# Filling a constant in 55 steps and bringing gamma over GpSimd's queue, in an RMSNorm and SiLU kernel

## The chip, the cores and the metric

The kernel runs on one core of a Trainium2 chip. The metric is the device time of one execution in microseconds. Three runs of the kernel before gave 316.87 to 317.08 us, with a median of 317.0 us.

## The reference

```
x: (8, 1024, 2048) f32, gamma: (2048,) f32, eps = 1e-5
rms = sqrt(mean(x ** 2, axis=-1) + eps)
out = gamma * x / rms
return out * (1 / (1 + exp(-out)))
```

Each of the 8192 rows of 2048 elements is normalised by its root mean square, multiplied by gamma and put through SiLU. The input and the output are 67.1 MB each.

## The kernel before

The 8192 rows are cut into 16 blocks of 512 rows. A block is one tile `xt` of 128 partitions, with four rows of x (J = 4), or 32 KB, in each partition. Six such tiles rotate (BUFS = 6), so that a block's tile can be loaded again only when the store of the block six before is done. The results are written over the block's own tile.

For each block, the squares of each row are summed by ScalarE for one or two of the four rows (L77) and by VectorE for the others (L83). ScalarE takes the square root (L89), VectorE the reciprocal (L94), VectorE multiplies the block by gamma (L99), and ScalarE applies SiLU with the reciprocal as its scale (L104). After the first block, the square root and the reciprocal are made for two blocks at a time.

Loads are issued from ScalarE's queue (L56), stores from SP's (L106). The order of all instructions is written out by hand under `manual_schedule`, so each engine and each queue takes its work in the order of the source. From block 6 on, a load stands behind the first row of squares of the block two before it.

The start is what the change touches. Gamma must stand in all 128 partitions of the tile `g`, because VectorE multiplies by it. Its 8 KB are loaded to partition 0 of `g` over SP's queue (L113). VectorE fills the 128 x 128 tile `ones` (L110) and the tile `eps_t` (L111). TensorE multiplies a row of ones by gamma, in four matmuls of 512 columns, into the PSUM tile `junk_v` (L116); each is two passes in the profile. VectorE copies `junk_v` to `g` (L118). ScalarE has a small activation that reads one column of `ones` (L112) and a small copy of one column of `junk_v` (L119). The loads of blocks 0 and 1 are issued ahead of that last copy, and those of blocks 2 to 5 behind it:

```
load(1)
nc.vector.tensor_copy(out=g, in_=junk_v)
nc.scalar.copy(out=junk_a[:, 0:1], in_=junk_v[:, d - 1:d])
for b in range(2, BUFS):
    load(b)
```

`junk_v` is also where VectorE's sums of squares put their unused products, so these stand behind the copy as well.

Of the kernel before, what the change touches and what calls it, by code (L numbers as in the profile page):

```python
# [1 line left out]

# [4 lines left out]

ACT = mybir.ActivationFunctionType
ALU = mybir.AluOpType


@with_exitstack
def kernel(
    ctx: ExitStack,
    tc: tile.TileContext,
    x: bass.AP,
    gamma: bass.AP,
    eps: bass.AP,
    out: bass.AP,
):  # L20

    nc = tc.nc
    P = nc.NUM_PARTITIONS
    f32 = mybir.dt.float32
    x2 = x.flatten_outer_dims()
    o2 = out.flatten_outer_dims()
    n, d = x2.shape
    J = 4
    BUFS = 6
    nblk = n // (P * J)  # L30
    last = nblk - 1
    xb = x2.rearrange("(b p j) d -> b p (j d)", p=P, j=J)
    ob = o2.rearrange("(b p j) d -> b p (j d)", p=P, j=J)

    GROUPS = [(0,)] + [(b, b + 1) for b in range(1, last, 2)] + [(last,)]

    singles = ctx.enter_context(tc.tile_pool(name="singles", bufs=1))
    pool = ctx.enter_context(tc.tile_pool(name="pool", bufs=BUFS))
    small = ctx.enter_context(tc.tile_pool(name="small", bufs=3))
    psum = ctx.enter_context(tc.tile_pool(name="psum", bufs=1, space=bass.MemoryType.PSUM))  # L40

    Q = 4
    w = d // Q
    g = singles.tile([P, d], f32)
    eps_t = singles.tile([P, 1], f32)
    ones = singles.tile([P, P], f32)
    junk_a = psum.tile([P, d], f32, name="junk_a")
    junk_v = psum.tile([P, d], f32, name="junk_v")
    blocks, sums, scales, place = {}, {}, {}, {}
    for q in GROUPS:  # L50
        for k, b in enumerate(q):
            place[b] = (q, k * J)

    def load(b):
        xt = pool.tile([P, J * d], f32, name="xt")
        nc.scalar.dma_start(out=xt, in_=xb[b])  # L56
        blocks[b] = xt

    def row(b, j):
        return blocks[b][:, j * d:(j + 1) * d]  # L60

    def share(b):
        if b == last:
            return 1
        return 1 if b in ONE else 2

    ONE = (5, 9, 13)

    def total(b, j):
        q, at = place[b]  # L70
        if q not in sums:
            sums[q] = small.tile([P, J * len(q)], f32, name="ss")
        return sums[q][:, at + j:at + j + 1]

    def squares_scalar(b):
        for j in range(share(b)):
            nc.scalar.activation(out=junk_a, in_=row(b, j), func=ACT.Square, accum_out=total(b, j))  # L77
            if j == 0 and BUFS <= b + 2 < nblk and b >= J:
                load(b + 2)

    def squares_vector(b):
        for j in range(share(b), J):
            nc.vector.tensor_tensor_reduce(  # L83
                out=junk_v, in0=row(b, j), in1=row(b, j), scale=1.0, scalar=0.0,
                op0=ALU.mult, op1=ALU.add, accum_out=total(b, j))

    def root(q):
        rms = small.tile([P, J * len(q)], f32, name="rms")
        nc.scalar.activation(out=rms, in_=sums.pop(q), func=ACT.Sqrt, scale=1.0 / d, bias=eps_t)  # L89
        scales[q] = rms  # L90

    def invert(q):
        rstd = small.tile([P, J * len(q)], f32, name="rstd")
        nc.vector.reciprocal(out=rstd, in_=scales[q])  # L94
        scales[q] = rstd

    def by_gamma(b, lo=0, hi=J):
        part = blocks[b][:, lo * d:hi * d].rearrange("p (j d) -> p j d", d=d)
        nc.vector.tensor_mul(out=part, in0=part, in1=g.unsqueeze(1).to_broadcast([P, hi - lo, d]))  # L99

    def silu(b):
        q, at = place[b]
        for j in range(J):
            nc.scalar.activation(out=row(b, j), in_=row(b, j), func=ACT.Silu,  # L104
                                 scale=scales[q][:, at + j:at + j + 1])
        nc.sync.dma_start(out=ob[b], in_=blocks[b])  # L106

    with tc.manual_schedule():
        load(0)
        nc.vector.memset(ones, 1.0)  # L110
        nc.vector.memset(eps_t, float(eps))  # L111
        nc.scalar.activation(out=junk_a[:, 0:1], in_=ones[:, 0:1], func=ACT.Square)  # L112
        nc.sync.dma_start(out=g[0:1, :], in_=bass.AP(tensor=gamma.tensor, offset=gamma.offset, ap=[[d, 1], [1, d]]))  # L113
        for c in range(Q):
            cols = slice(c * w, (c + 1) * w)
            nc.tensor.matmul(junk_v[:, cols], ones[0:1, :], g[0:1, cols], start=True, stop=True)  # L116
        load(1)
        nc.vector.tensor_copy(out=g, in_=junk_v)  # L118
        nc.scalar.copy(out=junk_a[:, 0:1], in_=junk_v[:, d - 1:d])  # L119
        for b in range(2, BUFS):  # L120
            load(b)

        q = GROUPS[0]
        squares_scalar(0)
        squares_vector(0)
        root(q)
        by_gamma(0)
        invert(q)

        q = GROUPS[1]  # L130
        squares_scalar(1)
        squares_vector(1)
        silu(0)
        squares_scalar(2)
        squares_vector(2)
        root(q)
        by_gamma(1)
        invert(q)
        by_gamma(2)
        silu(1)  # L140

        for q in GROUPS[2:-1]:
            a, c = q
            if a == 3:
                squares_scalar(a)
                silu(a - 1)
            else:
                silu(a - 1)
                squares_scalar(a)
            squares_vector(a)  # L150
            by_gamma(a)
            squares_scalar(c)
            squares_vector(c)
            root(q)
            invert(q)
            by_gamma(c)
            silu(a)

        q = GROUPS[-1]
        silu(last - 1)  # L160
        squares_scalar(last)
        squares_vector(last)
        root(q)
        by_gamma(last, 0, J // 2)
        invert(q)
        by_gamma(last, J // 2, J)
        silu(last)


# [1 line left out]
_INS = ['x', 'gamma', 'eps']  # L171
_OUTS = [((8, 1024, 2048), 'float32')]

_NUMBERS = {'eps': 9.999999747378752e-06}


# [26 lines left out]
```

## Time and profile before

| | |
|---|---|
| median of three runs | 317.0 us (316.87 to 317.08) |
| profiled execution, its time | 317.02 us |
| profiled execution, its span | 315.2 us |
| VectorE busy | 226.5 us, 72% of the span |
| ScalarE busy | 204.8 us, 65% |
| TensorE, GpSimd busy | 7.2 us, 0.2 us |
| DMA | 134.24 MB, mean 426 GB/s |
| a load, 4096 KB, from issue to landing | 38.6 us (median) |
| a store, 4096 KB, from issue to landing | 36.9 us (median) |

The span runs from the first instruction to the last; the profiled execution's time is longer by 1.8 us, which lie around the span. All durations in the text are from this one execution. A line such as L116 is a line of the kernel's file. The engines are PE (TensorE), PEld (its weight loads), DVE (VectorE), ACT (ScalarE), POOL (GpSimd) and SP (SyncE); a q behind the name means the engine's queue of instructions or transfers.

### The profile page before, as it was taken

The numbers are of one execution on the slowest core, as the hardware profiler recorded it, in microseconds if no ns is written. First come the engines' busy times: TensorE is split into PE (matmuls) and PEld (weight loads), VectorE is DVE, ScalarE is ACT, GpSimd is POOL, SyncE is SP. The second block draws the span as 40 slices with busy tenths as digits, with TensorE's granted clock in tenths as the row PEclk, the third lists the DMA queues.
The fourth block names the chain that finished last, engine by engine and source line by source line (L and its number), as shares of the span: only waits on it lengthen the run. The fifth ranks groups of instructions, "written<-read, shape, count | busy, mean of one in ns | idle before, by whom it ended". The sixth has DMA issues, their size and how long they took to land.

```text
span 315.2 us, 407 instructions
## 1 busy us (share of the span) xinstructions
PE 7.2 (2%) x8; PEld 2.5 (1%) x8; DVE 226.5 (72%) x101; ACT 204.8 (65%) x150; POOL 0.2 (0%) x4
## 2 busy tenths in 40 slices
PE   6200000000000000000000000000000000000000
PEld 2000000000000000000000000000000000000000
DVE  0699999997798584685949669466795957859400
ACT  1169959977970699606993079950899108995800
POOL 0000000000000000000000000000000000000000
DMA  8999999999999999999999999999999999999997
GB/s 334 407 457 412 412 437 403 462 403 463 403 457 407 457 407 462 403 458 407 457 407 457 412 453 412 457 407 457 412 453 412 453 412 453 420 449 416 449 424 308
DMA packets 4612, 134.24 MB, mean 426 GB/s; under 512 B 513, under 2 KB 513, under 8 KB 513
## 3 DMA queue, kind: packets, MB, share of 16 engines
q10 hardware_dynamic: 2304, 67.11, 49.8%
q1 hardware_dynamic: 2306, 67.12, 49.3%
q14 instruction: 2, 0.02, 0.0%
HBM read 67.12 MB, written 67.11 MB: 426 GB/s over the span
## 4 chain that ended last, share of the span: by engine, by line
DMA 68%; ACT 11%; DVE 11%; PE 2%; issue 1%; ACTq 1%; another core or an unknown queue 0%; DVEq 0%
DMA xt<-in_x_dram 68%; ACT xt L104 9%; DVE xt L99 5%; DVE junk_v L83 4%; PE junk_v L116 2%; ACT junk_a L77 1%; DVE g L118 1%; DMA g<-in_gamma_dram 1%; ACTq L198 1%; ACT L104 0%; ACT L89 0%; DVE ss L83 0%; ACT rms L89 0%; DVE rstd L94 0%
## 5 line engine op out<-in xcount | busy, mean ns | idle before, releaser
L99 DVE TENSOR_TENSOR xt<-xt,g 128x8192 f32<-128x8192 f32 (+1 forms) x17 | 138.9, 8170 | 6.9 <-ACT junk_a L77 6.6
L104 ACT ACTIVATE xt<-xt,rstd 128x2048 f32<-128x2048 f32 x64 | 122.3, 1989 | 5.3 <-DVE rstd L94 4.8
L83 DVE CUSTOM_DVE_ANT_0 junk_v<-xt 128x2048 f32<-128x2048 f32 x36 | 82.7, 2299 | 41.2 <-DMA xt<-in_x_dram 40.5
L77 ACT ACTIVATE junk_a<-xt 128x2048 f32<-128x2048 f32 x28 | 52.5, 1875 | 69.4 <-DMA xt<-in_x_dram 67.2
L89 ACT ACT_TABLE_LOAD x9 | 11.5, 1283 | 7.9 <-DVE ss L83 7.9
L104 ACT ACT_TABLE_LOAD x9 | 11.5, 1283 | 0.2
L94 DVE RECIPROCAL rstd<-rms 128x8 f32<-128x8 f32 (+1 forms) x9 | 1.7, 194 | 10.2 <-ACT rms L89 10.2
L118 DVE COPY g<-junk_v 128x2048 f32<-128x2048 f32 x1 | 2.3, 2292 | 9.1 <-PE junk_v L116 9.1
L116 PE MATMUL junk_v<-g,ones 1*128 1x512 f32 x8 | 7.2, 1072 | 2.9 <-DMA g<-in_gamma_dram 2.9
L119 ACT COPY junk_a<-junk_v 128x1 f32<-128x1 f32 x1 | 0.1, 144 | 9.9 <-DVE g L118 9.9
L77 ACT ACTIVATION_READ_ACCUMULATOR junk_a<-xt 128x1 f32 x28 | 5.2, 187 | 0.0
L83 DVE DVE_READ_ACCUMULATOR2_ANT ss<- 128x1 f32 x36 | 5.1, 140 | 0.0
L89 ACT ACTIVATE rms<-ss,eps_t 128x8 f32<-128x8 f32 (+1 forms) x9 | 2.7, 300 | 0.1
L116 PEld LDWEIGHTS junk_v<-g,ones 1*128 1x128 f32 x8 | 2.5, 325 | 6.0 <-issue 6.0
L112 ACT ACT_TABLE_LOAD x1 | 1.3, 1283 | 1.1 <-PEq L184 1.1
L110 DVE MEMSET ones<- 128x128 f32 x1 | 0.2, 165 | 0.8 <-PEq L184 0.8
L112 ACT ACTIVATE junk_a<-ones 128x1 f32<-128x1 f32 x1 | 0.2, 174 | 0.0
L184 POOL MEMSET const-bfloat16-1.0<- 128x1 bf16 x1 | 0.1, 101 | 0.0
L184 POOL MEMSET const-uint8-127<- 128x1 uint8 x1 | 0.1, 101 | 0.0
L184 POOL MEMSET const-float32-0.0<- 128x1 f32 x1 | 0.1, 98 | 0.2 <-issue 0.2
L184 POOL MEMSET const-float32-1.0<- 128x1 f32 x1 | 0.1, 98 | 0.0
L111 DVE MEMSET eps_t<- 128x1 f32 x1 | 0.1, 59 | 0.0
## 6 DMA issues: line engine op xcount, KB each, us to landing
xt<-in_x_dram ACTq DMA_DIRECT2D x16, 4096.0 KB, 38.6
out_dram<-xt SPq DMA_DIRECT2D x16, 4096.0 KB, 36.9
g<-in_gamma_dram SPq DMA_DIRECT2D x1, 8.0 KB
```

Source lines behind the costliest of these rows:

```text
L77: nc.scalar.activation(out=junk_a, in_=row(b, j), func=ACT.Square, accum_out=total(b, j))
L83: nc.vector.tensor_tensor_reduce(out=junk_v, in0=row(b, j), in1=row(b, j), scale=1.0, scalar=0.0, op0=ALU.mult, op1=ALU.add, accum_out=tot ...
L89: nc.scalar.activation(out=rms, in_=sums.pop(q), func=ACT.Sqrt, scale=1.0 / d, bias=eps_t)
L94: nc.vector.reciprocal(out=rstd, in_=scales[q])
L99: nc.vector.tensor_mul(out=part, in0=part, in1=g.unsqueeze(1).to_broadcast([P, hi - lo, d]))
L104: nc.scalar.activation(out=row(b, j), in_=row(b, j), func=ACT.Silu, scale=scales[q][:, at + j:at + j + 1])
L110: nc.vector.memset(ones, 1.0)
L112: nc.scalar.activation(out=junk_a[:, 0:1], in_=ones[:, 0:1], func=ACT.Square)
L116: nc.tensor.matmul(junk_v[:, cols], ones[0:1, :], g[0:1, cols], start=True, stop=True)
L118: nc.vector.tensor_copy(out=g, in_=junk_v)
L184: nc = _bacc.Bacc("TRN2", target_bir_lowering=False, num_devices=1)
L198: with _tile.TileContext(nc) as tc:
```

## The change

VectorE fills `ones` with one memset of 20 columns and 54 memsets of 2 columns; the memset of `eps_t` stands behind the first of them. Gamma is issued from GpSimd instead of SP, and goes as four pieces of 512 elements to partitions 0, 32, 64 and 96 of a new tile `g4`. The four matmuls take their piece of gamma, and the row of ones beside it, from these four partitions. Everything behind them is as it was.

```
+    g4 = singles.tile([P, w], f32)
...
         load(0)
-        nc.vector.memset(ones, 1.0)
+        nc.vector.memset(ones[:, 0:20], 1.0)
         nc.vector.memset(eps_t, float(eps))
+        for c in range(20, P, 2):
+            nc.vector.memset(ones[:, c:c + 2], 1.0)
         nc.scalar.activation(out=junk_a[:, 0:1], in_=ones[:, 0:1], func=ACT.Square)
-        nc.sync.dma_start(out=g[0:1, :], in_=bass.AP(tensor=gamma.tensor, offset=gamma.offset, ap=[[d, 1], [1, d]]))
+        nc.gpsimd.dma_start(out=g4[0:P:P // Q, :],
+                            in_=bass.AP(tensor=gamma.tensor, offset=gamma.offset, ap=[[w, Q], [1, w]]))
         for c in range(Q):
             cols = slice(c * w, (c + 1) * w)
-            nc.tensor.matmul(junk_v[:, cols], ones[0:1, :], g[0:1, cols], start=True, stop=True)
+            k = slice(c * (P // Q), c * (P // Q) + 1)
+            nc.tensor.matmul(junk_v[:, cols], ones[k, :], g4[k, :], start=True, stop=True)
         load(1)
         nc.vector.tensor_copy(out=g, in_=junk_v)
```

## The prediction

> **What bounds the kernel now.** I read, in this order, the page's engine shares, the chain of waits that ended last, busy time by stretch, and the timeline of the first 45 us. The chain gives 68% of the span to the loads of x, with VectorE 72% and ScalarE 65% busy. But the chain also starts with gamma, the matmuls and the copy, and then charges one load with 19.77 us:
>
> ```profile
> 0.73 2.04 DMA g<-in_gamma_dram
> 2.77 0.14 issue
> 2.90 7.17 PE junk_v L116 x8
> 10.08 0.02 issue
> 10.10 2.30 DVE g L118
> ...
> 12.51 19.77 DMA xt<-in_x_dram
> ```
>
> (Columns: start, length, what.) That is block 2's load, and the question is whether it was transferring or queueing. The stretches answer it (columns: stretch, its length, busy time of PE, PEld, DVE, ACT and POOL, granted clock, DMA share, GB/s):
>
> ```profile
> 0.00:2.00 2.00, 0.00 (x0) 0.00 (x0) 0.17 (x2) 0.86 (x1) 0.20 (x4) 1.00 0.56 152
> 2.00:4.00 2.00, 1.09 (x2) 0.60 (x3) 0.00 (x0) 0.60 (x2) 0.00 (x0) 1.00 0.94 360
> ...
> 12.00:22.00 10.00, 0.00 (x0) 0.00 (x0) 8.61 (x6) 5.73 (x7) 0.00 (x0) 1.00 1.02 439
> 22.00:36.00 14.00, 0.00 (x0) 0.00 (x0) 13.44 (x9) 13.35 (x10) 0.00 (x0) 1.00 1.01 435
> 36.00:60.00 24.00, 0.00 (x0) 0.00 (x0) 23.86 (x10) 20.49 (x17) 0.00 (x0) 1.00 1.00 415
> 60.00:280.00 220.00, 0.00 (x0) 0.00 (x0) 163.82 (x69) 148.66 (x106) 0.00 (x0) 1.00 1.00 434
> 280.00:312.00 32.00, 0.00 (x0) 0.00 (x0) 14.72 (x9) 15.12 (x11) 0.00 (x0) 1.00 0.99 427
> ```
>
> The 16 DMA engines are full from about 4 us to 312 us, at 415 to 439 GB/s whatever VectorE and ScalarE do. 134.24 MB at 434 GB/s is 309.3 us; the other 5.9 us of the 315.2 us span are the start and the end, and 1.8 us lie outside the span (317.02 us for the profiled execution, 0.02 above the median of 317.0). So an edit changes the time only if it leaves DMA engines without work, or moves the first or last byte.
>
> The timeline places the loads (start, length, instruction, idle time before and its releaser):
>
> ```profile
> 0.82 0.17 DVE L110 MEMSET ones<- 128x128 f32 x1 [0.82 <-PEq L184]
> 0.94 0.06 DVE L111 MEMSET eps_t<- 128x1 f32 x1
> 1.21 0.39 ACTq L56 DMA_DIRECT2D xt<-in_x_dram  x1
> 2.90 7.16 PE L116 MATMUL junk_v<-g,ones 1*128 1x512 f32 x8 [2.90 <-DMA g<-in_gamma_dram]
> 12.51 1.82 ACTq L56 DMA_DIRECT2D xt<-in_x_dram  x4
> 13.02 2.30 DVE L83 CUSTOM_DVE_ANT_0 junk_v<-xt 128x2048 f32<-128x2048 f32 x1 [0.62 <-DMA xt<-in_x_dram]
> 22.59 1.88 ACT L77 ACTIVATE junk_a<-xt 128x2048 f32<-128x2048 f32 x1 [2.52 <-DMA xt<-in_x_dram]
> 32.42 2.30 DVE L83 CUSTOM_DVE_ANT_0 junk_v<-xt 128x2048 f32<-128x2048 f32 x1 [0.50 <-DMA xt<-in_x_dram]
> ```
>
> Blocks 0, 1 and 2 are first used at 13.02, 22.59 and 32.42, one load (4.19 MB, 9.7 us at 434 GB/s) apart. Loads 2 to 5, issued from 12.51, queued behind load 1. The trace's DMA packet records put load 1's last completion at 22.2. Load 0, issued at 0.73, completed at 12.53: 11.8 us for 9.7 us of data, so a load on an idle queue needs about 2.1 us of lead. Load 2 therefore has to be issued by 22.2 - 2.1 = 20.1 us, and there are 20.1 - 12.51 = 7.6 us of slack.
>
> **The change part by part.** The early chain now is: gamma lands at L, the matmuls take M, and load 2 is issued at I = L + M + 2.56, where 2.56 is the fixed remainder (copy 2.29, the rest hand-overs): 2.77 + 7.18 + 2.56 = 12.51.
>
> *The fill.* One memset of 165 ns becomes one of 20 columns and 54 of 2. A column costs (165 - 59)/127 = 0.83 ns, from the 128- and 1-column rows, so the first takes 75 ns and the others 60. Their pitch is not in the trace: at least 33 ns (GpSimd's four constants), at most 114 ns (start of L110 to start of L111), and I take their own 60 ns. 54 x 60 ns = 3.2 us, and the constant is ready at 0.82 + 0.08 + 0.06 + 3.2 = 4.2 us (2.7 to 7.1) instead of 1.0. VectorE has nothing else until the copy at 10.10. ScalarE's warm-up at L112 reads column 0; if it waits for the first piece only, the table load to 2.4 us still hides that, and if for all, it runs at 4.2 us with load 1 due only when load 0 is through at 12.5. Cost on the end: 0.
>
> *Gamma.* SP's queue loses one issue of 0.34 us; its next is the first store at 35.65. GpSimd's queue gains one behind its constants (done at 0.4 us) and holds nothing else until the closing barrier. No GpSimd-issued transfer is in the trace. Lower bound: the old row, 2.04 us from issue to landing, so L = 2.8. Upper bound, from the first store: it was issued at 35.65 onto a ring that had been idle, and its packets started at 39.92 to about 42, each DMA engine first finishing some four 32 KB load packets of 1.21 us. Gamma went ahead of load 0's first packets (1.64 against 1.76 us); a software issue probably falls behind them. So L is 0.73 + 1 (an assumed issue, three times the hardware row) + 4.3 to 6.3, plus one packet for the completion, 7 to 9.2. I take L = 8, because the engines are then loaded as at the first store.
>
> The Trainium skill ("SBUF — State Buffer", section "SBUF: two separate sides") says that GpSimd cannot write its descriptors while VectorE runs in its two-port mode. No row here shows it. If all small memsets blocked GpSimd, its issue would start after them, at 4.2, and L would be 4.2 + 1 + 6.3 = 11.5, which makes I 18.6 and costs nothing unless the matmuls are serial; the row's 0.83 ns a column does not look like a doubled rate.
>
> *Matmuls.* Eight passes, 0.85 us apart, make 7.18 us. The slices now lie at partitions 0, 32, 64 and 96 and write four PSUM banks. If nothing overlaps, M = 7.18. If the last pass of one slice runs beside the first of the next, five steps remain: 5 x 0.85 + 0.2 = 4.5; if all overlap, 2 x 0.85 + 0.2 = 1.9. I take 4.5, since the order of issue is unchanged and the two passes of one slice add into the same bank.
>
> *Sum.* I = 8 + 4.5 + 2.56 = 15.1, 2.6 us later than before and 5.0 us short of 20.1; the ends are 2.8 + 1.9 + 2.56 = 7.3 (with the constant's 4.2 in the place of L, 8.7) and 9.2 + 7.18 + 2.56 = 18.9. All queue behind load 1. VectorE starts block 0's squares about 2.3 us later; what is late next is the first store, 35.65 to about 38, and the loads, still queued, use its share of the DMA engines meanwhile. The same 134.24 MB follow at the same rate. Later margins are of the same size: store 1 is issued at 53.56 and store 0 lands at 59.4, load 6 is issued at 66.08 with load 5 running to 85.
>
> *First and last bytes.* Gamma's 8 KB packet held up one DMA engine, which finished load 0 at 12.53 against 12.43 for the next slowest, and load 0's first packets began 0.12 us behind gamma's. Taking it off is worth 0.1 to 0.25 us; four 2 KB packets with their completions give back about 0.1 (8 KB took 0.84 us, latency included). One more semaphore in the closing list costs 0.06 (its pairs are 0.06 apart). Net -0.1 us: 316.9.
>
> **The rivals.** *Gamma starves the load queue (slower).* From I = 20.1 on, every microsecond is an idle one of all DMA engines. With serial matmuls that needs L above 10.4; with M = 4.5, above 13.0. If the four pieces only get their turn when load 0 is through at 12.53, L is about 12.8, and serial matmuls give I = 22.5: 2.4 us late, 319.3. With M = 4.5 it is 19.9 and costs nothing. A first software issue with some extra microseconds of its own adds as many. Against it: the store waited four packets, not a load's eight, and after 42 us the packets of the two queues alternate one by one. For it: no row prices the software issue. 0.20. The Trainium skill ("DMA: Bandwidth & Descriptors", section "Queues, rings and completion order") states that an engine drains a packet of some 9 to 17 descriptors before it changes rows; that would be all eight of a load, but the alternation in the trace contradicts it.
>
> *The start shortens (faster).* The first 4 us move 1.02 MB where 434 GB/s would be 1.74: 1.6 us are lost. If load 0's data began 0.7 us sooner without gamma in the hardware path, the time would be 316.3. Only 0.12 us of that stands between gamma's first packet and x's. 0.09.
>
> *The edits don't do what they say* (the constant gates the matmuls, the row groups don't overlap): I stays below 18.9 by the sum, and the time at 316.9. Part of the forecast.
>
> **How the numbers follow.** 0.2% of 317.0 is 0.63 us, about what a measurement of this kernel can tell from no change. Within it lies everything with I below 20.1 + 0.6 and small start terms: 0.71. Above it 0.20, below it 0.09. The likeliest case's own range is 316.5 to 317.3. For 8 in 10 the range takes in part of the slower rival, up to 2 us of idle, and a little of the faster: 316.4 to 319.0.
>
> **What would show it.** Right: 431 to 439 GB/s in every stretch from 4 to 36 us, block 1 used at 22.5 and block 2 at 32.3 as before, the four loads issued between 9 and 20 us, the first store later or earlier by as much as the copy, the last packets at the same place. The matmuls' group shows M, the landing of gamma L, VectorE's first microseconds the pitch. Wrong: loads 2 to 5 issued after 20.1, a dip of DMA share between 20 and 26 us, block 2 late by the same amount and the span longer by it; or the same stretches unchanged and the end or the time outside the span longer by more than 0.6 us.

## The result, and the profile after

The changed kernel takes 317.76 us (median of 22 runs), the kernel before 317.03 us (22 runs); the ratio is 1.0019, with a 95% interval of 1.0013 to 1.0026. It is 0.7 us slower: the forecast of 316.9 us, no change or 0.1 us faster, was wrong, though the time lies inside the range. The single runs show it well: 19 of 22 before took 316.76 to 317.24 us and three 317.39 to 317.66; 19 of 22 after took 317.46 to 318.12 us and three 316.82 to 317.24.

The profiled execution after took 317.77 us, its span is 316.0 us, again 1.8 us less. So the loss lies inside the span. These are the lines of its timeline that answer to those shown of before (start, length, instruction, idle time before and its releaser):

```profile
0.82 0.07 DVE L111 MEMSET ones<- 128x20 f32 x1 [0.82 <-PEq L189]
0.88 1.55 DVE L114 MEMSET ones<- 128x2 f32 x54
1.23 0.67 POOL L116 DMA_DIRECT2D g<-in_gamma_dram  x1 [0.78 <-POOLq L189]
8.40 2.09 PE L121 MATMUL junk_v<-g,ones 1*128 1x512 f32 x8 [8.40 <-DMA g<-in_gamma_dram]
12.96 1.85 ACTq L57 DMA_DIRECT2D xt<-in_x_dram  x4
13.26 2.30 DVE L84 CUSTOM_DVE_ANT_0 junk_v<-xt 128x2048 f32<-128x2048 f32 x1 [0.42 <-DMA xt<-in_x_dram]
23.64 1.88 ACT L78 ACTIVATE junk_a<-xt 128x2048 f32<-128x2048 f32 x1 [3.09 <-DMA xt<-in_x_dram]
33.46 2.30 DVE L84 CUSTOM_DVE_ANT_0 junk_v<-xt 128x2048 f32<-128x2048 f32 x1 [1.06 <-DMA xt<-in_x_dram]
```

The fill, gamma, the matmuls and the four loads are where the sum could have them: loads 2 to 5 are issued at 12.96, 7 us before the DMA engines would run dry by the prediction's estimate (20.1). But blocks 1 and 2 are first used 1.05 and 1.04 us later than before (22.59 and 32.42), and block 0 only 0.24 us later. Something happened to load 1, which was issued at 1.2 us in both kernels. With block 1 the first store comes late too, issued at 36.70 instead of 35.65. The stretches of after (columns as above) show no idle DMA:

```profile
12.00:22.00 10.00, 0.00 (x0) 0.00 (x0) 8.58 (x6) 5.73 (x7) 0.00 (x0) 1.00 1.02 440
22.00:36.00 14.00, 0.00 (x0) 0.00 (x0) 12.87 (x9) 12.30 (x9) 0.00 (x0) 1.00 1.00 433
60.00:280.00 220.00, 0.00 (x0) 0.00 (x0) 164.88 (x71) 149.69 (x107) 0.00 (x0) 1.00 1.00 434
280.00:312.00 32.00, 0.00 (x0) 0.00 (x0) 14.61 (x9) 15.01 (x11) 0.00 (x0) 1.00 1.00 430
```

A mean over 16 engines hides what one of them does. In the packet records an engine can be followed, since each of its packets starts within some 10 ns of the end of the one before. Each load or store ends with one completion write from each of the 16 DMA engines, and the trace's DMA packet records give their times (us from the span's start, sorted):

```
load 1, before:      21.79 ... 22.10 22.13 22.23        median 22.01
load 1, after:       21.75 ... 22.27 22.38 23.15        median 22.12
last store, before: 313.24 ... 313.67 313.81 313.97     median 313.43
last store, after:  313.17 ... 313.91 314.08 314.78     median 313.32
```

After the change one engine ends load 1 by 0.77 us behind all others, and the last store by 0.70. The median engine is 0.1 us earlier at the end; the last one is 0.81 us later, which is the difference of the spans. Followed through the records, it is the same engine at both places. What hit that engine in load 1 is one packet of the queue "instruction" (q14). The first fence below is the queue table of before for 18 to 20 us, the second that of after for the same two microseconds, the third that of before for 134 to 135 us (queue, packets, MB, share of 16 engines; q10 carries the loads, q1 the stores):

```profile
q10 hardware_dynamic: 32, 1.05, 121.3%
```

```profile
q10 hardware_dynamic: 31, 1.02, 119.3%
q14 instruction: 1, 0.01, 1.0%
```

```profile
q1 hardware_dynamic: 15, 0.49, 115.9%
q10 hardware_dynamic: 1, 0.03, 7.6%
q14 instruction: 1, 0.01, 1.9%
```

Both kernels fetch 8 KB of instructions twice between the start and the last store: before at 78.49 and 134.21 us, after at 18.63 and 77.67 us. One stayed, one came forward by 116 us. At 18.63 the packet took 309 ns, and the x packet behind it on that DMA engine 1.79 us instead of 1.21: 0.89 us lost. At 134.21 the same two numbers were 309 ns and 1.56 us, 0.66 us lost.

That gives **theory A**: the 54 more instructions bring VectorE's next fetch forward, from a time when loads and stores both run to the load-only start; it sets back one DMA engine, and the slowest of the 16 sets the end. **Rivals**: B, the pieces and completions of GpSimd's queue delay the DMA engines; C, the later loads and first store cost it; and, formed later, D, 54 more instructions cost the same wherever they stand, and E, VectorE itself suffers from the early fetch and the DMA engine's loss is a bystander.

### The profile page after: what moved, and what is told of

Read it like the earlier page. It is cut to its first block, busy times and chain, and to the rows that moved or that the text cites. A ratio compares the mean times of both kernels' runs of the same rounds, so it can differ in the third digit from the quotient of the medians.

```text
span 316.0 us, 460 instructions
## 1 busy us (share of the span) xinstructions
PE 2.1 (1%) x8; PEld 0.5 (0%) x8; DVE 228.0 (72%) x155; ACT 204.7 (65%) x150; POOL 0.9 (0%) x5
## 2 busy tenths in 40 slices
DMA packets 4642, 134.24 MB, mean 425 GB/s; under 512 B 540, under 2 KB 540, under 8 KB 544
## 4 chain that ended last, share of the span: by engine, by line
DMA 70%; ACT 11%; DVE 11%; issue 1%; PE 1%; ACTq 1%; DVEq 0%; POOLq 0%
DMA xt<-in_x_dram 68%; ACT xt L105 9%; DVE xt L100 5%; DVE junk_v L84 4%; DMA g<-in_gamma_dram 2%; ACT junk_a L78 1%; DVE g L123 1%; PE junk_v L121 1%; ACTq L203 1%; ACT L105 0%; ACT L90 0%; DVE ss L84 0%; ACT rms L90 0%; DVE rstd L95 0%; DVEq L203 0%
## 5 line engine op out<-in xcount | busy, mean ns | idle before, releaser
L121 PE MATMUL junk_v<-g,ones 1*128 1x512 f32 x8 | 2.1, 1133 | 8.4 <-DMA g<-in_gamma_dram 8.4
L114 DVE MEMSET ones<- 128x2 f32 x54 | 1.6, 60 | 0.0
L116 POOL DMA_DIRECT2D g<-in_gamma_dram x1 | 0.7, 668 | 0.8 <-POOLq L189 0.8
L121 PEld LDWEIGHTS junk_v<-g,ones 1*128 1x128 f32 x8 | 0.5, 307 | 8.4 <-issue 8.4
```

The lines of the kernel that those rows point to most:

```text
L114: nc.vector.memset(ones[:, c:c + 2], 1.0)
L116: nc.gpsimd.dma_start(out=g4[0:P:P // Q, :], in_=bass.AP(tensor=gamma.tensor, offset=gamma.offset, ap=[[w, Q], [1, w]]))
L121: nc.tensor.matmul(junk_v[:, cols], ones[k, :], g4[k, :], start=True, stop=True)
```

## The experiments

Each kernel was timed against the kernel before on the same chip, in five rounds. Fetch times are from each kernel's profiled execution.

**The queue alone.** The change with one memset again:

```
+        nc.vector.memset(ones, 1.0)
-        nc.vector.memset(ones[:, 0:20], 1.0)
-        for c in range(20, P, 2):
-            nc.vector.memset(ones[:, c:c + 2], 1.0)
```

> The change with VectorE's fill as one memset again; gamma stays on GpSimd's queue in four pieces. Theory A (the 54 more VectorE instructions pull the fetch of VectorE's next 8 KB of instructions from 134 us forward to 18.6 us, where only the load queue is at work and it costs one DMA engine 0.89 us instead of 0.31, and that engine ends last): the fetch is back near 134 us, load 1 completes within 0.5 us on all engines, 316.8 to 317.1 us, ratio 0.999 to 1.001. Theory B (the pieces and completions of the software queue delay the DMA engines): 317.6 to 317.8 us, ratio 1.002, with the fetch near 134 us. Theory C (loads 2 to 5 and the first store come later): ratio 1.002 too, if they are still late.

Measured 316.97 against 316.96 us, ratio 0.9999 (0.9991 to 1.0008). The queue table for 133 to 134 us has the fetch back:

```profile
q1 hardware_dynamic: 4, 0.13, 32.5%
q10 hardware_dynamic: 3, 0.10, 22.7%
q14 instruction: 1, 0.01, 1.9%
```

Loads 2 to 5 are issued at 12.77, late as in the change, and block 1 is used at 22.68. B falls, and so do C's later loads: queue, pieces and hand-overs stay, the loss goes. The first store is issued at 35.73, early as before, so this run says nothing on C's other half, the late store. (The late fetch is taken at 0.31 us in the expectation, its own time; with the gap behind it it is 0.66.)

The profiled execution of this kernel took 317.40 us, the highest of its eleven, and it too ends with one engine alone, at 314.40 with the next at 313.66; that engine is the one of the fetch at 133.42. So such an end also comes up now and then without an early fetch. Whether the three high runs of the kernel before are of this kind isn't shown.

**The fill alone.** The kernel before with the change's 55 memsets, gamma on SP's queue.

> The kernel before with VectorE's fill in 55 pieces; gamma stays on SP's queue in one piece, the matmuls as before. Theory A: an instruction fetch between 15 and 25 us, one engine's completion of load 1 some 0.6 to 0.9 us behind the others, 317.5 to 317.9 us, ratio 1.0015 to 1.003. Theory B: 317.0 us, ratio 1.000, whatever the fetch does. Theory C: 317.0 us, since the copy is at its old place.

Measured 317.77 against 316.96 us, ratio 1.0017 (1.0007 to 1.0028): the whole loss. The queue table for 18 to 20 us, and the timeline's line of block 1's first use:

```profile
q10 hardware_dynamic: 28, 0.92, 107.9%
q14 instruction: 1, 0.01, 1.0%
```

```profile
23.42 1.88 ACT L77 ACTIVATE junk_a<-xt 128x2048 f32<-128x2048 f32 x1 [2.75 <-DMA xt<-in_x_dram]
```

One engine loses 0.87 us to the fetch at 18.43; it ends load 1 at 22.93, the next at 22.50, and it ends the last store, at 314.85, with the next at 314.13. As A said.

**Fewer pieces.** The change with `for c in range(20, P, 4)`, 27 memsets of four columns.

> The change with the 108 columns filled in 27 memsets of 4 columns instead of 54 of 2. Theory A: VectorE's fetch falls between 55 and 80 us, where loads and stores both run, and costs its engine 0.3 us: 316.9 to 317.2 us, ratio at most 1.0007. Theory B and theory C: as the change itself, 317.6 to 317.8 us, since queue, pieces and hand-overs are the same.

Measured 317.14 against 316.96 us, ratio 1.0003 (0.9994 to 1.0012), with the fetch at 64.21. No loss can be told, as A said.

**ScalarE's fetch instead.** The kernel before, with more ScalarE work ahead of the copy:

```
         load(1)
+        for _ in range(46):
+            nc.scalar.activation(out=junk_a[:, 0:1], in_=ones[:, 0:1], func=ACT.Square)
```

> The kernel before with 46 more small activations of one column on ScalarE behind load 1's issue, in ScalarE's idle time before 12.5 us; VectorE, gamma and the matmuls as before. Theory A: ScalarE's own fetch comes forward from 78.5 us to between 14 and 26 us, one engine ends load 1 or load 2 some 0.6 to 0.9 us behind the others, and the time is 317.4 to 317.9 us. Theories B and C: 317.0 us, if the activations end before the copy.

Measured 317.37 against 316.96 us, ratio 1.0010 (1.0001 to 1.0018). VectorE's fetch is at 134.19 as before; ScalarE's came from 78.5 to 19.37. The queue table for 19 to 21 us:

```profile
q10 hardware_dynamic: 29, 0.95, 110.7%
q14 instruction: 1, 0.01, 1.0%
```

Here the engine lost 0.57 us, less than expected, and in the profiled execution it was one that had been ahead, so the completions of load 1 show no engine far behind. The profiled execution took 317.11 us, near the kernel before, so it isn't typical of the runs. The time rose by half as much as with VectorE's fetch, 0.03 us short of the range expected, and the interval begins just above 1. ScalarE's longer code also brings a third fetch, at 230.09, on the same DMA engine, which cost it another 0.42 us. So this run fits A with another engine's instructions, but it is weak evidence.

**The same instructions, late.** The kernel before with 54 memsets of an unused tile ahead of the last group:

```
+        for c in range(54):
+            nc.vector.memset(pad[:, 2 * c:2 * c + 2], 1.0)
         q = GROUPS[-1]
```

> The kernel before with 54 memsets of two columns of an unused tile on VectorE ahead of the last group, where VectorE waits for the last load; the start is as before. Theory A (the place in time of VectorE's instruction fetch decides, not the number of instructions): the fetch stays at 134 us, 316.9 to 317.2 us, ratio 0.9995 to 1.0007. Theory D (54 more instructions cost the same wherever they stand): 317.6 to 317.9 us.

Measured 317.07 against 317.13 us, ratio 0.9998 (0.9990 to 1.0007), the fetch at 134.23. D falls: 54 more instructions cost nothing here, so their place decides.

**46, 35 and 108 pieces.** The change with the fill cut otherwise: 46 and 35 pieces of two columns behind a longer first memset, and 108 of one.

> The change with 46 pieces of two columns instead of 54, behind a first memset of 36 columns. Theory A: VectorE's fetch falls between 20 and 36 us, while only loads run and before the first store; it costs its DMA engine about 0.87 us, one completion of load 2 or 3 stands alone by 0.5 us or more, 317.5 to 317.9 us, ratio 1.0012 to 1.0028. Theory D: between 1.0003 (27 pieces) and 1.0019 (54), by the count about 1.0014.

> The change with 35 pieces of two columns behind a first memset of 58 columns. Theory A: VectorE's fetch falls between 45 and 60 us, once loads and stores both run; it costs its engine about 0.6 us, and the time is 316.9 to 317.3 us, ratio at most 1.0008. Theory D: by the count between 27 and 54 pieces, about 1.0008 to 1.001, 317.3 us.

> The change with 108 pieces of one column instead of 54 of two. Theory A: VectorE's fetch falls between 4 and 12 us, in the load-only stretch, and a second one past 150 us; 317.5 to 318.0 us, no more than with 54 pieces, ratio 1.0012 to 1.003. Theory D: twice the change's cost, 318.2 us, ratio 1.0038.

| pieces | VectorE's fetches, us | time, us | ratio (95%) |
|---|---|---|---|
| 108 | 6.14 and 193.73 | 318.40 | 1.0035 (1.0022 to 1.0049) |
| 54 (the change) | 18.63 | 317.76 | 1.0019 (1.0013 to 1.0026) |
| 46 | 23.08 | 317.64 | 1.0014 (1.0005 to 1.0023) |
| 35 | 37.72 | 317.15 | 0.9998 (0.9989 to 1.0007) |
| 27 | 64.21 | 317.14 | 1.0003 (0.9994 to 1.0012) |
| 1 (queue alone) | 133.42 | 316.97 | 0.9999 (0.9991 to 1.0008) |

Two expectations missed. With 35 pieces the fetch came at 37.7, just behind the first store's issue and ahead of its packets, not at 45 to 60; its engine lost 0.94 us, and the time did not rise. So what counts is not the bare loss but what is left of it once the stores have begun: between 37 and 41 us every engine's packets take about 1 us longer in all, and that engine's loss fell into this. With 108 pieces the time is 0.4 us above A's range, and near D's number (318.2). Its trace shows why: on the engine that ends last (315.42, the next 313.67) lies also the second fetch, which costs 0.67 us; without it that engine would end at 314.75, as after the change. The order of these times would fit D too; the late fill and the 35 pieces do not.

With 46 pieces the first store is issued at 35.83, as early as in the kernels without the loss, and the time is 0.14% longer all the same: the late first store, the other half of C, isn't needed for a loss. Here the fetch delays block 2 and with it the second store (54.20 instead of 53.56), and no run separates that from the lag of the engine. Against a delay of the whole kernel stands its end after the change, where the median engine is not late.

The engine that the early fetch set back is the one that ends last after the change, in the fill alone and with 108 pieces. With 46 pieces it is another: the engine of the fetch ends at 313.83, and the last, at 314.73, is one that no fetch had hit; between 37 and 43 us its packets took 2.1 us longer in all, those of the others 0.6 to 1.0.

**One packet put there by hand.** To get a lag without any fetch, 6 KB of gamma were loaded once more to one partition of an unused tile, at the start and late.

```
+        nc.vector.memset(pad[0:1, 0:1], 0.0)
+        nc.sync.dma_start(out=pad[0:1, :], in_=...)    # the first 1536 elements of gamma
```

> The kernel before with 6 KB of gamma loaded once more, over SP's queue to one partition of an unused tile, behind a one-element memset of that tile that follows the copy at 12.4 us. No instruction is moved to another 8 KB. Theory A (any transfer of a few KB on one DMA engine costs that engine much more than its bytes while one queue of 32 KB packets runs, and an engine that is behind when the stores begin stays behind to the end): VectorE's fetch stays near 134 us, the extra packet falls between 13 and 20 us, its engine loses 0.5 to 0.9 us, 317.3 to 317.9 us. Theory E (VectorE's stream itself suffers from the early fetch, and the DMA engine's loss is a bystander): 317.0 us, ratio 1.000.

> The same extra 6 KB load, but behind VectorE's work for block 4, past 70 us, while loads and stores both run. Theory A: the extra packet costs its engine 0.4 to 0.7 us and the time is 316.9 to 317.4 us, clearly under that of the load at 13 us. Theory E: 317.0 us.

Measured 317.01 against 317.01 us (1.0000, 0.9991 to 1.0009) and 317.10 (1.0002, 0.9993 to 1.0010). Both tell little: the packet, at 15.79 and at 138.17, took 0.23 us and the next x packet its usual 1.21. That refutes a part of A as it stood: these 6 KB cost their engine their own time and no more. A gap behind the packet, 0.11 to 0.63 us, was seen behind the instruction fetches only.

**Four and three such packets.** So the lag has to be built from several.

> The kernel before with 6 KB of gamma loaded four times more, one after the other, to one partition of an unused tile over SP's queue, from 12.4 us on. All four fall on one DMA engine and cost it 0.23 us each, 0.94 us in all, before the first store's packets at about 40 us. Theory A (a DMA engine that is about 0.9 us behind when the stores begin is still that far or further behind at the end, and the slowest of the 16 sets the time; the instruction fetch is only one way to get there): 317.4 to 318.1 us, ratio 1.001 to 1.003. Theory E (what costs is in VectorE's early fetch itself, apart from the time it takes on a DMA engine): 317.0 us, ratio 1.000.

> The same four extra loads, but behind the third store's issue at 65 us, while loads and stores both run. If an engine's lag only adds up, wherever it arises: as the early loads, 317.4 to 317.9 us. If the beginning of the stores makes a lag worse (theory A with that addition): less than the early loads by 0.3 to 0.6 us, 317.0 to 317.5 us. Theory E: 317.0 us.

> The kernel before with 6 KB of gamma loaded three times more over SP's queue, one after the other on one DMA engine, behind the issue of loads 2 to 5: 0.70 us on one engine before 36 us, with loads 2 to 5 still issued by 14.5 us. Theory A with the addition (a lag of one engine grows when the stores begin): 317.4 to 318.0 us, ratio 1.0012 to 1.003, more than the three late loads by 0.3 us or more. Plain adding up: 317.1 to 317.4 us, as the late loads. Theory E: 317.0 us.

> The same three loads behind the third store: 0.70 us on one engine between 70 and 120 us. Both forms of theory A: 317.1 to 317.4 us, ratio 1.0003 to 1.0012 (four gave 317.44). Theory E: 317.0 us.

Four early loads gave 319.09 us (1.0068, 1.0042 to 1.0095), but they moved more than one engine's lag: the loads of x share completion counters with them, and the issue of loads 2 to 5 stretched to 5.6 us. The late loads lay behind the third store on SP's queue and held up the fourth, from 83.19 to 111.59 and 106.33 us; four of them gave 317.44 us (1.0015, 1.0006 to 1.0024), three gave 318.84 with single runs from 317.21 to 321.30 (1.0058, 1.0037 to 1.0079). Four early and three late loads missed what A had for them. These three kernels can't be read for the lag.

The three early loads, put behind the issue of loads 2 to 5, can. From their timeline:

```profile
12.47 1.81 ACTq L57 DMA_DIRECT2D xt<-in_x_dram  x4
13.19 2.30 DVE L84 CUSTOM_DVE_ANT_0 junk_v<-xt 128x2048 f32<-128x2048 f32 x1 [0.83 <-DMA xt<-in_x_dram]
23.38 1.88 ACT L78 ACTIVATE junk_a<-xt 128x2048 f32<-128x2048 f32 x1 [3.40 <-DMA xt<-in_x_dram]
33.26 2.30 DVE L84 CUSTOM_DVE_ANT_0 junk_v<-xt 128x2048 f32<-128x2048 f32 x1 [1.44 <-DMA xt<-in_x_dram]
```

Loads 2 to 5 are issued as before, blocks 1 and 2 come 0.8 us late (1.05 after the change), and VectorE's fetch is at 134.24. Three packets at 16.29, 21.36 and 26.44 cost one engine 0.70 us. The time is 317.49 against 316.97 us, ratio 1.0016 (1.0008 to 1.0025). So three packets that set back one of 16 DMA engines by 0.7 us make this kernel slower with VectorE's fetch at its old place: a loss of this size needs no early fetch, and E isn't needed to explain it. The engine of the three packets ends at 314.14, 0.69 behind the median engine and later than any engine before (313.97), so its lag lasts to the end. But it isn't the last: that is the engine of the fetch at 77.91, at 314.32, which had also lost time at the stores' beginning. So the trace gives the lag a part of the loss, and the rest stays open.

No version beat the kernel before.

## Why the prediction was wrong, point by point

**What bounds the kernel**: right, and not fine enough. The DMA engines are full, so "an edit changes the time only if it leaves DMA engines without work, or moves the first or last byte". (From 4 to 12 us, a stretch left out of its fence, the rate was 397 GB/s, not 415 to 439; after the change it was 419.) The last byte belongs to one engine, and I read "first and last bytes" only at the start of gamma and at the closing list.

**The fill: the step that failed.** It said "Cost on the end: 0", counting 54 instructions as VectorE time, and that part held: they took 1.55 us (28.2 ns apart, under my lower bound of 33) and hid behind gamma. But each instruction also moves the point at which VectorE's next 8 KB are fetched. The page of before shows two instruction packets, and the prediction gives them no term. The moved fetch goes with 0.81 us on the last completion (0.73 us in the medians of the time), which can be split from the packet records:

- The fetch cost 0.89 us instead of 0.66: 0.23.
- The engine that it hit was 0.16 us behind the median before it. The one at 134 us was 0.12 ahead of the median without it (313.97 - 0.66 = 313.31 against 313.43): 0.28.
- From load 1 to the end the lag behind the median grew from 1.04 to 1.46 us: 0.42. From 46 us on this engine has no slow packet, so the growth lies around the beginning of the stores; by 60 us it had begun 46 packets of 32 KB, every other engine 47.
- The median engine ended 0.11 us earlier: -0.11.

The first and the second I take as shown for this execution. Why the lag grew stays open. In the three early loads the lag of the engine of the packets did not grow (1.00 us behind the median at load 2, 0.69 at the end), and with 46 pieces it was another engine than the one with the fetch that came out of the stores' beginning one packet short. So the last part of the way, from an engine that is late when the stores begin to the late end, is seen in three traces and not explained. Nor is it shown why the gap behind an instruction fetch is 0.58 us while only loads run and 0.35 later.

**Gamma**: right. L was forecast at 8 and was 8.27, 7.04 us from an issue that waited to 1.23 us. Its four pieces started at 6.04 to 6.56, behind some four x packets, and the completions came up to 7.85. The Trainium skill's two rules that spoke against the change ("SBUF — State Buffer", section "SBUF: two separate sides", and "DMA: Bandwidth & Descriptors", section "Queues, rings and completion order") did not show here: GpSimd's issue began at 1.23 and took 0.67 us beside the 54 memsets, and at 1.22 and 0.67 without them; and the pieces did not wait for the end of load 0 at 12.69. Whether the memsets run in the two-port mode of which the first rule speaks, no run shows.

**Matmuls**: mis-sized on the safe side. M was 2.1 us, near the lower end (1.9), not 4.5: the eight passes took about what the forecast gives two (1.9), so the four slices ran beside one another.

**The sum of the start**: I was 8.27 + 2.12 + 2.56 = 12.95 (12.96 in the trace), not 15.1. The slack to 20.1 us covered it, as argued; the rival of a starved load queue did not occur.

**First and last bytes**: the gain of 0.1 us isn't shown. The median engine ended 0.11 us earlier, but with the fill alone, where gamma has its old place, it ended 0.18 earlier; and the queue alone, with gamma moved, took the time of the kernel before.

**What would prove it wrong**: of the list's two cases the second came true: the stretches from 12 us on move what they did (440, 433, 434 and 430 GB/s), and the end is 0.8 us later. Block 2 was 1.04 us late as well, but not through loads issued after 20.1, as the first case has it. The list held no cause for either.

## What to carry to other kernels

In this kernel, with the DMA engines full, the time was that of the slowest of 16, not of their mean: read the completions of each, and ask of any edit whether it sets back a single one. Added instructions shifted in time the fetch of an engine's code, and the fetch ran on the same DMA engines as the data; so read the instruction queue's packets by time, and try the same number of instructions in another place before you explain a small difference by what they compute.

## What the runs showed of the hardware that I had not expected

- VectorE's first fetch in the kernel came when it had started some 60 instructions of the profile (59 before 134.21 us, 58 with 27, 35 and 46 pieces, 65 before 18.63), and moved with their number: 64.2 us with 27 pieces, 6.1 with 108. With 108 pieces 112 had started by then; what sets the place exactly isn't shown. An 8 KB fetch set its DMA engine back by 0.42 to 0.94 us, a 6 KB data packet by 0.23.
- The eight matmul passes, each with one row of ones and one of gamma, took 2.09 us with the rows in four groups of partitions, and 7.16 with all in partition 0.
- Two-column memsets follow one another every 28.2 ns (1.55 us for 54), though each shows 60 ns.
